# Moving the streamed tiles of the down and output projections by 64 bytes in SBUF

## The chip, the cores and the metric

The kernel runs on one core of a Trainium2 chip. The metric is device time in microseconds (us) of one execution; lower is better.

## What is computed

Two transformer blocks in a row on one sequence of 256 tokens with 1,024 features, all in float32. Cut to what matters here:

```python
def swiglu(h, w_gate, w_up, w_down):            # D_FF = 2816
    return (silu(h @ w_gate) * (h @ w_up)) @ w_down

def first_block(x, ...):                        # DEPTH = 2
    for i in range(DEPTH):
        x = x + 0.5 * swiglu(rms_norm(x, g[0]), ...)
        h = rms_norm(x, g[1])
        x = x + (even_mixer(h, ...) if i % 2 == 0 else mla_mixer(h, ...))
        x = x + 0.5 * swiglu(rms_norm(x, g[2]), ...)
        x = x + per_layer_embedding(rms_norm(x, g[3]), p[i], ...)
    return x

def second_block(x, ...):                       # one hybrid layer
    u = rmsnorm(x, g) @ w_in
    x = x + concat([attention(u), ssd(u), pooling(u)]) @ w_out
    x = x + swiglu(rmsnorm(x, g2), ...)
    return rmsnorm(x, norm_final)
```

Five feed-forward layers (SwiGLU) hold most of the arithmetic. Each of the three mixers ends in an output projection of 1,024 by 1,024.

## The kernel before

Activations lie transposed: a tile has 128 features on the partitions and the 256 tokens along the free dimension, so `x` is eight tiles of 128x256. Weights (220 pieces of 1 MB) stream from HBM through three buffers `wraw`, in the order in which they are used.

**Split operands.** Every float32 operand of a large product is split into two tiles of the type fp32r, a high part and the remainder. A product is then three matmuls that accumulate into the same PSUM region: high weight by high row, high weight by low row, low weight by high row. `load_piece` (lines 233 to 260) makes `whi` on ScalarE (line 256) and `wlo` on VectorE (line 257), half a piece at a time. Each buffer of `whi` and `wlo` is 128x1024, that is eight weight blocks of 128 columns (512 bytes per partition each).

**What is stationary and what streams.** All the matmuls of the large products go through `mm` (line 163). In `fm` (lines 327 to 385) and `out_proj` (lines 400 to 411) a 128x128 weight block is loaded as the stationary operand (a LDWEIGHTS instruction, engine PEld in the rows) and the 256 columns of a row tile stream past it (a MATMUL, engine PE). In `tm` (lines 387 to 398) it is the other way round: a block of the row tile is stationary and the weights stream, 512 columns at a time in most cases.

**Which row tiles there are.**
- `hh0` to `hh7` and `hl0` to `hl7`, the high and low parts of the normalized rows. They are the moving operand of the gate and up projections of all five feed-forward layers (1,056 matmuls each) and of the first projections of the mixers.
- `big`, a rotating set of 13 tiles of 128x1024. The gated rows of a feed-forward are written there, two blocks (high, low, high, low) to a tile (lines 445 to 450), and are the moving operand of the down projection: 22 blocks by 8 output blocks by 3, 528 matmuls per layer. The even mixer's output projection (8 by 8 by 3, 192 matmuls), the two small projections of the per-layer embedding (48 each) and five of the eight blocks of the hybrid layer's output projection (120) stream from `big` too.
- `o2`, three tiles of 128x512 with the rows of one attention head or pair (named `o` in the rows): the moving operand in the output projection of the attention layer (192) and in the other three blocks of the hybrid layer's (72).

**Addresses.** Three pools take SBUF one after the other: `wp` (weights), `cp` (constants, `x`, `hh`, `hl`), `sp` (working tiles). Inside a pool tiles are laid out in the order in which a name is first asked for, each rounded up to 32 bytes:

```python
        self.wp = pool("wp")          # L114
        self.cp = pool("cp")
        self.sp = pool("sp", 2)
        ...
        t = self.sp.tile([P, cols], dt, name="big", bufs=13)     # L129
```

From the sizes follow these byte addresses within a partition (the same on all 128):

| tiles | first address | bytes of one | start of every 512-byte block, modulo 512 |
|---|---|---|---|
| `whi`, `wlo` | 41,088 and 65,664 | 4,096 | 128 |
| `hh0`, `hl0`, ... `hl7` | 99,648 | 1,024 | 320 |
| `gu` (first name of `sp`) | 132,352 | 2,048 | 256 |
| `big` | 153,344 | 4,096 | 256 |
| `o2` | 209,664 | 2,048 | 256 |

So a streamed `hh` or `hl` tile starts 192 bytes behind a weight block, modulo 512, and a streamed `big` or `o2` tile 128 bytes behind one, whatever buffer and whatever block it is.

**Order around the change.** A framework schedules each engine's instructions and sets the semaphores. The order of the matmuls follows the code: in a feed-forward, two column pairs are accumulated block by block while the rows are still being normalized (the first 96 matmuls), the sum of squares is taken with four small matmuls on `sqa` (`Stat.begin`, line 69), 48 matmuls later two transposes of `ny` spread its inverse root over the partitions (`Stat.finish`, line 88), and the rest of gate and up follows without another kind of matmul; the down projection comes right behind.

Of the kernel before, what the change touches and what calls it, by code (L numbers as in the profile page):

```python
# [10 lines left out]
FT = mybir.dt.float32  # L11
# [6 lines left out]
P = 128  # L18
# [88 lines left out]
class Kern:  # L107
# [61 lines left out]
    def constants(self):  # L169
        nc, a, cp = self.nc, self.a, self.cp  # L170
        self.cols = cp.tile([P, a["cols"].shape[1]], FT, name="cols")
        self.x = []
        self.raw = [self.wp.tile([P, PIECE], FT, name="wraw", bufs=3) for _ in range(2)]

        def load_x(c, n, eng=nc.sync):
            t = cp.tile([P, n * T], FT, name=f"x{c}")
            eng.dma_start(t, a["xT"][:, c * T : (c + n) * T])
            self.x += [t[:, u * T : (u + 1) * T] for u in range(n)]

        def load_w(i, q, n):  # L180
            o = slice(q * 512, (q + n) * 512)
            nc.sync.dma_start(self.raw[i][:, o], a["wts"][i][:, o])


        self.ones = cp.tile([P, 1], FT, name="ones")
        nc.vector.memset(self.ones, 1.0)
        idle = self.tmp(512, "gu", bufs=3)
        nc.vector.memset(idle, 0.0)
        ps = self.aux()
        for _ in range(5):  # L190
            self.mm(ps[:, :T], idle[:, :P], idle[:, :T])
        load_x(0, 1)
        nc.scalar.dma_start(self.cols, a["cols"])
        load_w(0, 0, 1)
        load_x(1, 1, nc.scalar)
        load_w(0, 1, 1)
        load_x(2, 1, nc.scalar)
        load_w(0, 2, 1)
        load_x(3, 1)
        load_w(0, 3, 1)  # L200
        load_x(4, 2)
        load_w(1, 0, 2)
        load_x(6, 2)
        load_w(1, 2, 2)
        self.ident = cp.tile([P, P], FT, name="ident")
        nc.sync.dma_start(self.ident, a["ident"])
        self.hT = [
            (cp.tile([P, T], FR, name=f"hh{c}"), cp.tile([P, T], FR, name=f"hl{c}"))
            for c in range(D)
        ]  # L210
        self.eps = cp.tile([P, 1], FT, name="eps")
        nc.vector.memset(self.eps, EPS)
        nc.scalar.activation(self.tiny(1, "nz"), self.ones, AF.Silu)
# [1435 lines left out]
```

## Time and profile before

| | |
|---|---|
| median of 3 runs | 1348.85 us (1342.49 to 1348.98) |
| the profiled execution's own time | 1348.33 us |
| its span, first to last instruction | 1346.5 us |
| TensorE busy with matmuls | 1319.8 us of the span, 10,830 instructions |
| TensorE busy with weight loads | 1290.1 us (beside the matmuls) |
| VectorE, ScalarE, GpSimd busy | 920.6, 727.1, 76.7 us |
| read from HBM | 232.78 MB, 174 GB/s over the span |

The busy time of a matmul in the profile reaches from its issue to its modelled end, and the next one is issued long before that; so neither "busy" nor the mean duration of one (281 ns and the like) is the time that a matmul costs. In a stretch that holds matmuls of one kind and no pause, that cost is the step from one start to the next. It is had from a stretch of known length: the length, plus the duration of one (0.28 us, because matmuls that only reach into the stretch are counted as well), divided by the count.

### The profile page before, as it was taken

The numbers are of one execution on the slowest core, as the hardware profiler recorded it, in microseconds if no ns is written. First come the engines' busy times: TensorE is split into PE (matmuls) and PEld (weight loads), VectorE is DVE, ScalarE is ACT, GpSimd is POOL, SyncE is SP. The second block draws the span as 40 slices with busy tenths as digits, with TensorE's granted clock in tenths as the row PEclk, the third lists the DMA queues.
The fourth block names the chain that finished last, engine by engine and source line by source line (L and its number), as shares of the span: only waits on it lengthen the run. The fifth ranks groups of instructions, "written<-read, shape, count | busy, mean of one in ns | idle before, by whom it ended". The sixth has DMA issues, their size and how long they took to land.

```text
span 1346.5 us, 25894 instructions
## 1 busy us (share of the span) xinstructions
PE 1319.8 (98%) x10830; PEld 1290.1 (96%) x10830; DVE 920.6 (68%) x1528; ACT 727.1 (54%) x1110; POOL 76.7 (6%) x94
## 2 busy tenths in 40 slices
PE   8999999999999999999999899999998999999997
PEld 8999999899999999999999679999998998999997
DVE  6866567968667557866656767766558897866643
ACT  6655446546544456655445666544445675644442
POOL 4000010002000001000010002000002000200001
PEclk9999999999999999999999999999999999999998
DMA  8755455345555453655455324555545343555541
GB/s 313 261 192 205 175 191 186 103 159 182 188 187 198 171 205 126 220 188 188 160 187 193 118 72 148 189 188 188 183 163 188 126 167 119 185 188 188 188 159 61
DMA packets 34933, 235.50 MB, mean 175 GB/s; under 512 B 4016, under 2 KB 4784, under 8 KB 7168
## 3 DMA queue, kind: packets, MB, share of 16 engines
q1 hardware_dynamic: 32976, 229.98, 49.1%
q0 software_dynamic: 832, 2.47, 0.6%
q8 instruction: 85, 1.39, 0.4%
q10 hardware_dynamic: 1008, 1.40, 0.3%
q14 instruction: 32, 0.26, 0.1%
HBM read 232.78 MB, written 1.05 MB: 174 GB/s over the span
## 4 chain that ended last, share of the span: by engine, by line
PE 74%; DVE 5%; ACT 2%; issue 1%; DVEq 0%; ACTq 0%
PE acc L163 70%; PE aux L163 4%; DVE wlo L257 2%; PE aux L299 0%; DVE big L1172 0%; PE aux L1127 0%; ACT whi L256 0%; DVE qs L958 0%; DVE kv L958 0%; DVE big L511 0%; ACT ae L1119 0%; ACT big L946 0%; ACT at L1129 0%; DVE big L1494 0%; DVE nz L293 0%
## 5 line engine op out<-in xcount | busy, mean ns | idle before, releaser
L257 DVE TENSOR_TENSOR wlo<-wraw,whi 128x1024 fp32r<-128x1024 f32 (+1 forms) x440 | 530.3, 1219 | 270.1 <-ACT whi L256 177.0
L256 ACT ACTIVATE whi<-wraw 128x1024 fp32r<-128x1024 f32 (+1 forms) x440 | 451.7, 1048 | 319.3 <-PE acc L163 224.9
L163 PE MATMUL acc<-hh,whi 128*128 128x256 f32 x2192 | 330.7, 281 | 4.1 <-ACT hh L535 3.1
L163 PE MATMUL acc<-hl,whi 128*128 128x256 f32 x2192 | 329.6, 280 | 0.2 <-DVE hl L540 0.2
L163 PE MATMUL acc<-hh,wlo 128*128 128x256 f32 x2192 | 328.8, 280 | 0.2 <-DVE wlo L257 0.2
L163 PEld LDWEIGHTS acc<-hh,whi 128*128 128x128 f32 x2192 | 288.5, 189 | 5.8 <-ACT hh L535 3.8
L163 PEld LDWEIGHTS acc<-hh,wlo 128*128 128x128 f32 x2192 | 288.7, 189 | 0.8 <-DVE wlo L257 0.6
L163 PEld LDWEIGHTS acc<-hl,whi 128*128 128x128 f32 x2192 | 288.6, 189 | 0.4 <-DVE hl L540 0.4
L163 PE MATMUL acc<-big,whi 128*128 128x256 f32 x2032 | 277.9, 283 | 0.0
L163 PEld LDWEIGHTS acc<-big,whi 128*128 128x128 f32 x2032 | 261.6, 189 | 0.4 <-ACT big L267 0.2
L163 PE MATMUL acc<-big,wlo 128*128 128x256 f32 x1016 | 164.8, 283 | 0.0
L163 PEld LDWEIGHTS acc<-big,wlo 128*128 128x128 f32 x1016 | 139.8, 189 | 0.0
L315 POOL TENSOR_TENSOR sqa<-sqa,sq 128x256 f32<-128x256 f32 x72 | 65.5, 910 | 1135.8 <-ACT sq L314 1133.7
L426 DVE TENSOR_TENSOR gu<-acc,rb 128x512 f32<-128x512 f32 (+1 forms) x122 | 81.9, 678 | 51.9 <-PE acc L163 51.9
L270 ACT ACTIVATE hh<-x,cols 128x256 fp32r<-128x256 f32 x64 | 30.3, 503 | 84.2 <-DVE x L465 80.6
L267 ACT ACTIVATE big<-pr 128x256 fp32r<-128x256 f32 x114 | 45.9, 409 | 51.9 <-DVE pr L444 50.1
L442 ACT ACTIVATE sg<-gu 128x256 f32<-128x256 f32 x110 | 44.8, 411 | 38.7 <-DVE gu L426 38.5
L268 DVE TENSOR_TENSOR big<-pr,big 128x256 fp32r<-128x256 f32 x114 | 47.9, 426 | 20.3 <-ACT big L267 20.2
L444 DVE TENSOR_TENSOR pr<-sg,gu 128x256 f32<-128x256 f32 x110 | 45.4, 418 | 2.8 <-ACT sg L442 2.8
L271 DVE SCALAR_TENSOR_TENSOR hl<-x,cols,hh 128x256 fp32r<-128x256 f32 x64 | 36.9, 602 | 8.5 <-ACT hh L270 8.3
L163 PE MATMUL aux<-big 128*128 128x128 f32 (+5 forms) x260 | 37.6, 310 | 1.9 <-DVE big L680 1.7
L314 ACT ACTIVATE sq<-x 128x256 f32<-128x256 f32 x62 | 24.0, 405 | 24.9 <-DVE x L467 18.4
(297 smaller groups left out, 788.1 us busy)
## 6 DMA issues: line engine op xcount, KB each, us to landing
wraw<-wts SPq DMA_DIRECT2D x216, 1024.0 KB, 4.9
wraw<-wts SPq DMA_DIRECT2D x4, 256.0 KB, 5.0
wraw<-wts SPq DMA_DIRECT2D x2, 512.0 KB, 6.5
x<-xT SPq DMA_DIRECT2D x2, 256.0 KB, 5.7
big<-wsT POOLq DMA_DIRECT2D x1, 512.0 KB, 10.4
gu<-pT ACTq DMA_DIRECT2D x2, 256.0 KB, 3.1
out<-big SPq DMA_DIRECT2D x2, 256.0 KB, 2.2
out<-big ACTq DMA_DIRECT2D x2, 256.0 KB, 2.4
```

Source lines behind the costliest of these rows:

```text
L163: return self.nc.tensor.matmul(out, l, r, start=start, stop=stop, skip_group_check=True).ins
L256: nc.scalar.activation(hi[:, i], s, AF.Copy)
L257: nc.vector.tensor_tensor(lo[:, i], s, hi[:, i].bitcast(FT), op=OP.subtract)
L267: a = nc.scalar.activation(hi, src, AF.Copy)
L268: b = nc.vector.tensor_tensor(lo, src, hi.bitcast(FT), op=OP.subtract)
L270: a = nc.scalar.activation(hi, src, AF.Copy, scale=scale)
L271: b = nc.vector.scalar_tensor_tensor(lo, src, scale, hi.bitcast(FT), op0=OP.mult, op1=OP.subtract)
L314: nc.scalar.activation(q, src, AF.Square)
L315: self.mark = nc.gpsimd.tensor_tensor(self.sq[0], self.sq[0], q, op=OP.add).ins
L426: self.nc.vector.tensor_tensor(out.rearrange("p (u t) -> p u t", u=n), ps.rearrange("p (u t) -> p u t", u=n), rb.unsqueeze(1).to_broadcast ...
L442: self.mark = nc.scalar.activation(sg, gu[:, :T], AF.Silu).ins
L444: nc.vector.tensor_tensor(pr, sg, gu[:, T:], op=OP.mult)
```

## The change

One tile of 64 bytes per partition is asked for in the working pool, after `gu` and before every other name of that pool. Nothing reads or writes it.

```diff
@@ -208,6 +208,8 @@
             (cp.tile([P, T], FR, name=f"hh{c}"), cp.tile([P, T], FR, name=f"hl{c}"))
             for c in range(D)
         ]
+
+        self.sp.tile([P, 16], FT, name="pad", bufs=1)
         self.eps = cp.tile([P, 1], FT, name="eps")
         nc.vector.memset(self.eps, EPS)
         nc.scalar.activation(self.tiny(1, "nz"), self.ones, AF.Silu)
```

Every tile of `sp` but `gu` lies 64 bytes further on: `big` starts at 153,408 and `o2` at 209,728, both 320 modulo 512, and so do `sq`, `sqa`, `sg`, `pr`, `rb`, `ny`, `ae`, `at` and the other working tiles move by 64. The tiles of `wp` and `cp` (the weights, `x`, `hh`, `hl`, `ident`, the constants) stay where they were. A streamed `big` or `o2` tile now starts 192 bytes behind a weight block, modulo 512. The instructions of every engine and their order are the same as before.

## Rows read from the trace of the kernel before

**Rows 1.** The page: the span, and each engine's busy time.
```profile
span 1346.5 us, 25894 instructions
...
PE 1319.8 (98%) x10830; PEld 1290.1 (96%) x10830; DVE 920.6 (68%) x1528; ACT 727.1 (54%) x1110; POOL 76.7 (6%) x94
```
**Rows 2.** The page's costliest groups: busy us, mean ns | idle before, releaser.
```profile
L257 DVE TENSOR_TENSOR wlo<-wraw,whi 128x1024 fp32r<-128x1024 f32 (+1 forms) x440 | 530.3, 1219 | 270.1 <-ACT whi L256 177.0
...
L163 PE MATMUL acc<-big,whi 128*128 128x256 f32 x2032 | 277.9, 283 | 0.0
...
L163 PE MATMUL acc<-big,wlo 128*128 128x256 f32 x1016 | 164.8, 283 | 0.0
...
L444 DVE TENSOR_TENSOR pr<-sg,gu 128x256 f32<-128x256 f32 x110 | 45.4, 418 | 2.8 <-ACT sg L442 2.8
```
**Rows 3.** Stretches, PE alone: from:to, length, busy (count), granted clock, DMA share, GB/s.
```profile
40.00:120.00 80.00, 80.00 (x708) 1.00 0.63 218
132.00:190.00 58.00, 58.00 (x491) 1.00 0.52 182
216.00:236.00 20.00, 20.00 (x179) 1.00 0.61 211
...
340.00:420.00 80.00, 80.00 (x682) 1.00 0.54 185
435.00:495.00 60.00, 60.00 (x502) 1.00 0.49 170
...
950.00:1005.00 55.00, 55.00 (x461) 1.00 0.51 176
...
1276.00:1332.00 56.00, 56.00 (x469) 1.00 0.36 129
```
**Rows 4.** Timeline, PE, hybrid layer: weights stream past stationary rows. Start us, length, ...
```profile
1106.34 1.07 PE L163 MATMUL acc<-whi,hh 128*128 128x256 f32 x8
...
1109.06 1.07 PE L163 MATMUL acc<-whi,hh 128*128 128x256 f32 x8
```
**Rows 5.** Timeline, PE, start of the second feed-forward.
```profile
313.40 1.75 PE L163 MATMUL acc<-hh,wlo 128*128 128x256 f32 x14
314.99 0.50 PE L163 MATMUL aux<-ones,sqa 128*128 128x1 f32 x4
...
316.38 1.10 PE L163 MATMUL acc<-hl,whi 128*128 128x256 f32 x8
...
320.15 1.10 PE L163 MATMUL acc<-hh,wlo 128*128 128x256 f32 x8
```
**Rows 6.** Timeline, PE, first feed-forward, just behind its two transposes.
```profile
27.44 1.07 PE L163 MATMUL acc<-hl,whi 128*128 128x256 f32 x8
28.34 0.84 PE L163 MATMUL acc<-hh,wlo 128*128 128x256 f32 x6
```
**Rows 7.** Groups in the stretch 129.8 to 192.5 us: the first down projection.
```profile
L163 PE MATMUL acc<-big,whi 128*128 128x256 f32 x352 | 45.5, 281 | 0.0
L163 PE MATMUL acc<-big,wlo 128*128 128x256 f32 x176 | 25.6, 281 | 0.0
```
**Rows 8.** Groups of the whole span by shape: `o2` streamed; stationary `big`, 512 columns.
```profile
L163 PE MATMUL acc<-o,whi 128*128 128x256 f32 x176 | 34.2, 290 | 0.4 <-ACT o L267 0.4
...
L163 PE MATMUL acc<-whi,big 128*128 128x512 f32 x68 | 19.3, 405 | 1.7 <-DVE nz L293 1.1 <-DVE nz L292 0.6
```
**Rows 9.** Timeline, PE, 512 columns: past stationary `hh` and past stationary `big`.
```profile
206.19 2.00 PE L163 MATMUL acc<-whi,hl 128*128 128x512 f32 x8
208.03 1.99 PE L163 MATMUL acc<-wlo,hh 128*128 128x512 f32 x8
...
759.54 1.56 PE L163 MATMUL acc<-whi,big 128*128 128x512 f32 x6
760.94 0.86 PE L163 MATMUL acc<-wlo,big 128*128 128x512 f32 x3
```
**Rows 10.** Instructions on `ident`: transposes, ns min/median/max.
```profile
L1127 PEld LDWEIGHTS aux<-ident,ae x42: 137/140/143, 782.4 to 1131.7; 128*128 128x128 f32 x42
```

## The prediction

> **What bounds the kernel now.** The page comes first: TensorE is busy for 1319.8 of 1346.5 us [rows 1], so what a change is worth is what it takes from TensorE's stream of matmuls. The groups come next: 2,032 and 1,016 matmuls stream `big` [rows 2], and 176 stream `o2` past `whi` [rows 8], with half as many (88) past `wlo`. That is 3,312 matmuls with a moved tile, all 128x256. The groups give a mean of 283 ns each, which is overlap and no cost. The cost is in the view by stretches, which I read third: length plus 0.28 us, by the count.
>
> - Gate and up of the first feed-forward, `hh` and `hl` streamed: 80.28 us by 708 is 113.4 ns a matmul; its down projection, `big` streamed: 58.28 by 491 is 118.7 ns [rows 3].
> - Gate and up of the second feed-forward: 80.28 by 682 is 117.7 ns; its down projection: 60.28 by 502 is 120.1 ns. The fourth and fifth down projections: 55.28 by 461 is 119.9 ns and 56.28 by 469 is 120.0 ns [rows 3].
>
> TensorE has no idle time in any of these stretches and its clock is granted in full (1.00, the 2.4 GHz level), so neither a wait nor the clock makes the differences. The reader is to see two of them. One goes with the tile: 118.7 against 113.4, 120.0 against 117.7. The other goes with time: the same `hh` tiles against the same buffers take 113.4 ns in one stretch and 117.7 in another. I call these the **short** and the **long pace**.
>
> The pace changes where a stream is interrupted. In the second feed-forward 14 matmuls before the four on `sqa` take 1.59 us, 113.6 ns each; behind these four, 32 matmuls take 3.77 us, 117.8 ns each [rows 5], and that stays so for the stage. In the first feed-forward the pace behind the two transposes is the short one (8 in 0.90 us, about 113 ns [rows 6]). A down projection follows its gate and up without a pause and is at its own shorter pace (118.7) behind the short one and at its longer (120.0) behind the long one. So I read four numbers: tiles at distance 192 take 113.4 or 117.7, tiles at distance 128 take 118.7 or 120.0, and the pace is inherited.
>
> **Is it the distance?** Three other readings have to go first. That streaming from the region of `hh` is quick in itself: in the hybrid layer `whi` streams past stationary `hh`, 24 matmuls in 2.72 us, 113.3 ns [rows 4], so a tile of another pool at another offset streams just as quickly when its partner is `hh`. That it is the order of the matmuls: gate and up go through eight row blocks, the down projection through 22, and 118.7 and 120.0 stand there alike. That it is streaming alone: with `big` stationary and weights streaming 512 columns, 6 matmuls take 1.40 us, 233 ns, against 8 in 1.84 us, 230 ns, with `hh` stationary [rows 9]; the pair is the slower one in that direction too. What all quick pairs share is 192 bytes (or its reverse) and all slow pairs 128. What no row separates is that every slow pair has a tile of the working pool in it.
>
> **The change, part by part.**
>
> 1. *Removed and added instructions:* none, on any engine, and none moves; so no queue, wait or DMA is dealt with differently.
>
> 2. *The streamed tiles.* Taken at the pace that `hh` has at the same distance, each stage keeping the short or long pace that it is in:
>  - first down projection, 352 + 176 = 528 matmuls [rows 7], 118.7 to 113.4: 528 x 5.3 ns = 2.8 us;
>  - second down projection with the small projection of 48 behind it, 576, 120.1 to 117.7: 576 x 2.4 = 1.4 us;
>  - the other three down projections, 1,584, 120.0 to 117.7: 1,584 x 2.3 = 3.6 us;
>  - the even mixer's output projection, 192, which no long stretch of mine covers: it starts anew behind a pause, as the blocks do that take the short pace, so 192 x 5.3 = 1.0 us (0.4 at the long one);
>  - the remaining 432 (192 of the attention layer, 192 of the hybrid layer, 48 of the second small projection), cut up by transposes and scores: between 432 x 2.3 = 1.0 and 432 x 5.3 = 2.3 us, 1.6 taken. What of it lies under a head's softmax chain is worth nothing, so the low end is 0.
>
>  These sum to 10.4 us. In all the down projections TensorE's time is the path itself (no idle), and what follows each starts when its last matmul ends.
>
> 3. *Stationary `big`, 512 columns* (68 with `whi` streaming [rows 8], 34 with `wlo`): 102 x 3 ns = 0.3 us, 0 if hidden.
>
> 4. *Transposes.* `ident` stays and `ae`, `big`, `o` move under it. Their weight loads spread from 137 to 143 ns [rows 10]; the 42 of that row are the largest of several groups, some 150 in all, so up to 150 x 6 ns = 0.9 us either way. Taken as 0: at 128 columns nothing shows which relation is the worse.
>
> 5. *VectorE, ScalarE, GpSimd.* Pairs of operands change their relation too, such as `pr<-sg,gu`, where `sg` moves and `gu` stays (418 ns, 110 times [rows 2]). I know of no row that prices this. It is hidden under TensorE in the streams: `wlo` takes 1.22 us [rows 2] for eight weight blocks, which TensorE uses up in 24 matmuls or 2.7 us at 113.4 ns. Were 10 ns on each of the 110 uncovered, it would be 1.1 us. Taken as 0.
>
> 6. *The feed.* A down projection at 113.4 ns needs 64 KB per three matmuls, 65,536 B in 340 ns, 193 GB/s. The stretch of 40 to 120 us runs at that pace with 218 GB/s moved [rows 3], so the DMA follows.
>
> Sum: 10.4 + 0.3 = 10.7 us. Made against the profiled execution's own 1348.33 us, that is 1337.6 us; the median of the runs shown is 0.5 us higher, so I say **1338 us**, 0.8% under 1348.85. With the bounds of parts 2 to 5 the likeliest case reaches from 1334 to 1341.
>
> The Trainium skill speaks against all of it: "SBUF — State Buffer", section "Who interferes with whom", gives TensorE two independent read ports, one for the moving operand and one for the weight load, and says that PE never waits on anyone. By that rule the distance between the two operands could not matter, and the sum would be 0, 1348.3 us. The trace does not agree that nothing happens (113.4 against 118.7 ns in the same profile), but it does not show that the two reads are what collides.
>
> **The rivals.**
>
> - *The distance does nothing (chance 0.16).* The pace belongs to the working pool's place in SBUF, or to something else about these tiles. For it: no row parts pool from distance, and the rule just named. Against it: the quick stream of `whi` past `hh`, and the constancy of 118.7 and 120.0 over 13 buffers in 53 KB. That the change doesn't do what it says (the tile dropped, or rounded away) belongs here; 64 bytes are two of the allocator's steps of 32, so I give that next to nothing. Time: 1348.3 us, no change.
>
> - *More streams take the short pace (0.10).* The tiles around the interruptions (`sqa`, `ny`) move too, and the pace seems to be set by how a stream starts. If one of the four later feed-forwards turns, its gate and up gain 1,056 x 4.3 ns and its down projection as much for 528: 1,584 x 4.3 = 6.8 us, hence 1331 us; with all four, 1310. For it: the first feed-forward is in the short pace with the same code. One run of the three before is 6.4 us under the others, the size of one such turn. Against it: rows 5 have an entry that I see nothing of the move in, and the later four behave alike.
>
> - *The first feed-forward loses the short pace (0.08).* The same 6.8 us given back: 1344.5 us, within what counts as no change.
>
> - *Slower (0.04).* The distance does nothing and the move of `ny` and `sqa` turns the stretches that are short now into long ones. The place is the entry of a stream; the price is 4.3 ns for each `hh` matmul that is at the short pace: some 900 in the first feed-forward (103 us from its transposes to 129.8 us), some 350 in the even mixer, and the first 48 to 96 of every other stage, 600 in all; 1,850 x 4.3 = 8.0 us, and 1.4 ns (118.7 to 120.1) for the 720 matmuls of the first down projection and the even output, 1.0 us. That gives 1357.3 us, 0.6% slower. It decides only if nearly all these entries turn: 6.7 us, the bound of "slower", need over 1,500 matmuls.
>
> **How the numbers follow.** The forecast has 0.62. A measurement of this kernel can tell about 0.5%, 6.7 us, from no change; the forecast's 10.7 clears that by 4, and I take 0.02 of it as falling short through the scatter of the runs. Faster: 0.60 + 0.10 = 0.70. Same: 0.16 + 0.08 + 0.02 = 0.26. Slower: 0.04. The range takes in the likeliest case (1334 to 1341), one further turn of pace (1331), one lost (1344.5) and no effect at all (1348.3 to 1348.9): 1329 to 1349. Left out are several turns at once and the slower case, under 0.1.
>
> **What the profile of the changed kernel would show.** Right: the stretches of the down projections give about 113.4 ns behind a gate and up of 113.4 and about 117.8 behind 117.8, with no step where `big` takes over from `hh`; the stretches of gate and up are unchanged. The distance is refuted if the down projections stay at 118.7 and 120.0. If the total is off while these are right, the fault is in the inheritance: the stretches of gate and up from 30 to 130, 340 to 420, and those of the last three feed-forwards would show which pace each took. If TensorE shows idle time in a down projection, the feed was the limit after all.

## The result and the profile after

| | before | changed |
|---|---|---|
| median of 20 runs each | 1348.64 us | 1341.25 us |
| lowest to highest | 1342.49 to 1353.85 | 1331.63 to 1346.12 |
| the profiled execution, its span | 1348.33, 1346.5 | 1341.66, 1340.0 |

The ratio of the two sets of runs is 0.9936, with a 95% interval of 0.9918 to 0.9954: 8.6 us faster (6.2 to 11.1), 0.64%. The two medians alone lie 7.4 us apart. The forecast was 1338 us, faster by 10.7. A second set of runs of the same changed kernel, in the last experiments below, gave 0.9938 (0.9909 to 0.9967).

The page of the changed kernel, its span, its busy times and the two large groups that stream `big`, which answer to [rows 1, 2]:

```profile
span 1340.0 us, 25894 instructions
...
PE 1313.9 (98%) x10830; PEld 1283.5 (96%) x10830; DVE 922.5 (69%) x1528; ACT 727.4 (54%) x1110; POOL 76.7 (6%) x94
...
L163 PE MATMUL acc<-big,whi 128*128 128x256 f32 x2032 | 271.8, 280 | 0.0
...
L163 PE MATMUL acc<-big,wlo 128*128 128x256 f32 x1016 | 161.7, 280 | 0.0
```

The instructions are the same in number, the other engines are busy for as long as before, within 2 us, and TensorE still is for 98%. What changed is the pace. The view by stretches of the changed kernel, PE alone (columns as in [rows 3]: from:to, length, busy and count, granted clock, DMA share, GB/s):

```profile
40.00:120.00 80.00, 80.00 (x708) 1.00 0.63 216
132.00:188.00 56.00, 56.00 (x497) 1.00 0.54 189
...
340.00:420.00 80.00, 80.00 (x682) 1.00 0.55 190
430.00:490.00 60.00, 60.00 (x512) 1.00 0.51 178
...
950.00:1004.00 54.00, 54.00 (x460) 1.00 0.51 176
1270.00:1328.00 58.00, 58.00 (x495) 1.00 0.36 127
```

Length plus 0.28 us, by the count, as ahead of the prediction. Gate and up of the first two feed-forwards stand where they stood: 113.4 and 117.7 ns. The first down projection went from 118.7 to 113.2 ns, the second from 120.1 to 117.7, the fourth from 119.9 to 118.0, the fifth from 120.0 to 117.7. These are the short and the long pace, and each down projection has that of the gate and up ahead of it. The place where `big` takes over from `hh` shows no step any more. The timeline of the changed kernel there (start us, length us, engine, line, operation, tiles, shape, count):

```profile
128.22 1.07 PE L163 MATMUL acc<-hh,wlo 128*128 128x256 f32 x8
129.13 0.39 PE L163 MATMUL acc<-big,whi 128*128 128x256 f32 x2
...
129.47 0.39 PE L163 MATMUL acc<-big,whi 128*128 128x256 f32 x2
```

Eight with `hh` take 0.91 us, three with `big` 0.34: 113 ns on both sides of the takeover.

**Where the 6.5 us between the two spans come from.** The kernels have the same matmuls in the same order, so their starts can be paired. Counted from the first matmul of each part to the first behind it, the five down projections (with the 48 small matmuls behind the second) take 2.8, 1.3, 1.2, 1.2 and 1.2 us less, 7.6 in all. All matmuls that stream `big` or `o2`, these included, take 9.2 us less. Those that stream `hh` and `hl` take 0.3 less, the 512-column ones apart from the next paragraph 0.1 less. That would be 9.6; 3.0 us are given back at one place, and 0.1 among the small matmuls.

That place is the start of the attention layer, where `big` is stationary. First the timeline of the kernel before, then that of the changed one, at the same instructions:

```profile
740.23 1.43 PE L163 MATMUL acc<-whi,big 128*128 128x512 f32 x5
```

```profile
732.63 1.67 PE L163 MATMUL aux<-ones,gu 128*128 128x1 f32 x10
734.22 2.50 PE L163 MATMUL acc<-whi,big 128*128 128x512 f32 x5
```

Five matmuls of 512 columns reach over 1.43 us in the one and 2.50 in the other, and the clock says why. By stretches, the changed kernel (granted clock third from the end):

```profile
726.00:732.00 6.00, 6.00 (x55) 1.00 0.53 178
733.00:740.00 7.00, 7.00 (x22) 0.52 0.46 150
```

From about 733.3 us the clock is granted at 0.5, the 1.2 GHz level, until 740.1, and then in full again. Ahead of the fall TensorE had done two dozen matmuls of a single column (on `ones`; 14, then the 10 shown). The kernel before does the same ones and kept its clock of 1.00 in this execution. Such spells are not the change's own: all thirteen profiles, that of the kernel before included, have one at the start of the hybrid layer (6.8 or 10.2 us long) and one at their very end. A further one, of 3.4 or 6.8 us, is in eight of them, here or some 200 us earlier. The second profile of the changed kernel (e9) has it here too, from 733.3 us on, but 3.4 us long; those of the kernel before, e1, e2, e5 and e11 have none. So its length differs between executions of one kernel; whether its place does is not shown, and what sets one off was not tried.

### The profile page after: what moved, and what is told of

Read it like the earlier page. It is cut to its first block, busy times and chain, and to the rows that moved or that the text cites. A ratio compares the mean times of both kernels' runs of the same rounds, so it can differ in the third digit from the quotient of the medians.

```text
span 1340.0 us, 25894 instructions
## 1 busy us (share of the span) xinstructions
PE 1313.9 (98%) x10830; PEld 1283.5 (96%) x10830; DVE 922.5 (69%) x1528; ACT 727.4 (54%) x1110; POOL 76.7 (6%) x94
## 4 chain that ended last, share of the span: by engine, by line
PE 75%; DVE 4%; ACT 2%; issue 1%; DVEq 0%; ACTq 0%
PE acc L163 70%; PE aux L163 4%; DVE wlo L259 1%; ACT whi L258 0%; DVE big L1174 0%; PE aux L301 0%; PE aux L1129 0%; DVE qs L960 0%; ACT at L1131 0%; DVE big L1002 0%; ACT ae L1121 0%; ACT big L948 0%; DVE big L513 0%; DVE big L1496 0%; ACT hh L272 0%
## 5 line engine op out<-in xcount | busy, mean ns | idle before, releaser
L163 PE MATMUL acc<-big,whi 128*128 128x256 f32 x2032 | 271.8, 280 | 0.0
L163 PEld LDWEIGHTS acc<-big,whi 128*128 128x128 f32 x2032 | 256.6, 189 | 0.5 <-ACT big L269 0.2
L163 PE MATMUL acc<-big,wlo 128*128 128x256 f32 x1016 | 161.7, 280 | 0.0
## 6 DMA issues: line engine op xcount, KB each, us to landing
big<-wsT POOLq DMA_DIRECT2D x1, 512.0 KB, 10.7
```

The lines of the kernel that those rows point to most:

```text
L163: return self.nc.tensor.matmul(out, l, r, start=start, stop=stop, skip_group_check=True).ins
```

## The experiments

Theory D: the distance between the streamed tile and the weight block, modulo 512 bytes or a divisor of it, sets the price of a matmul. Theory R: the price belongs to the working pool, its region of SBUF, or to having been moved. Theory P stands beside D: which of the two paces a stream takes is set where it is entered, and inherited from then on. All edits below are shown against the changed kernel, but for that of e7, and cut to the lines that matter ("..." marks a cut); "pad" is the changed kernel's 64-byte tile. A number of ns per matmul is worked out from the stretch as above, or from two starts of a timeline. The kernels of e1, e2, e3, e6 and e7 were executed once each; with 11 us between executions of one kernel their times settle little, and it is their paces that carry the argument.

**e1. The same tiles, moved further, to a distance of 0 modulo 128.** `big` stands 256 bytes behind a weight block; a second tile in front of `o2` puts this one 320 bytes behind, 64 modulo 128.

```diff
-        self.sp.tile([P, 16], FT, name="pad", bufs=1)
+        self.sp.tile([P, 32], FT, name="pad", bufs=1)
...
+        self.sp.tile([P, 16], FT, name="opad", bufs=1)     # in front of o2
```

> The unused tile is 128 bytes instead of 64, and a second one of 64 bytes stands ahead of o2: big starts 256 bytes behind a weight block modulo 512 (0 modulo 128), o2 320 (64 modulo 128), hh and hl stay at 192. If the pace goes by the distance modulo 128: down projections at 118.7 behind a short-pace gate and up and 120.0 behind a long one, as before the change, with a step where big takes over; the attention layer's output projection (o2) at 113.3 or 117.8. If it goes by the place in the working pool, or by big having been moved at all: down projections at 113.3 or 117.8 again. If the period is 256 or 512: big differs from the kernel before, o2 from the changed one.

It took 1349.33 us (the kernel before beside it: 1348.67, median of 7). First and second down projection, by stretches:

```profile
132.00:190.00 58.00, 58.00 (x486) 1.00 0.52 182
...
435.00:495.00 60.00, 60.00 (x502) 1.00 0.49 170
```

119.9 and 120.1 ns: the gain is gone, though the tiles were moved and lie in the same pool. `o2` is the counterpart in the same kernel. Its matmuls in the attention layer's output projection, by the timeline of this kernel and then of the kernel before, first and last of a run of 36 steps:

```profile
818.76 0.40 PE L163 MATMUL acc<-o,whi 128*128 128x256 f32 x2
...
823.00 0.40 PE L163 MATMUL acc<-o,whi 128*128 128x256 f32 x2
```

```profile
818.28 0.41 PE L163 MATMUL acc<-o,whi 128*128 128x256 f32 x2
...
822.60 0.41 PE L163 MATMUL acc<-o,whi 128*128 128x256 f32 x2
```

4.24 us against 4.32, 117.8 ns against 120.0. In one program, from one pool, the tile at 64 modulo 128 is quick and the tile at 0 is slow: that is D, and R falls. One thing is off: behind a gate and up at 113.4 ns, `big` at 256 takes 119.9 ns and not the 118.7 that it takes at 128. So 128 and 256 are not quite alike.

**e2. The two kinds of tile exchange their distances.** A tile in front of `hh` in place of the pad moves `hh` to 256, `big` to 192, and `o2` to 448.

```diff
+        cp.tile([P, 16], FT, name="cpad")                  # in front of hh
...
-        self.sp.tile([P, 16], FT, name="pad", bufs=1)
...
+        self.sp.tile([P, 64], FT, name="opad", bufs=1)     # in front of o2
```

> An unused tile of 64 bytes ahead of hh0 in the constants' pool, and 256 bytes ahead of o2, none behind gu: hh and hl are at 256 (0 modulo 128), big at 192, o2 at 448 (64 modulo 128). If the distance decides: gate and up at 118.7 or 120.0 and down projections at 113.3 or 117.8, the reverse of the kernel before; with 6,576 matmuls on hh and hl about 15 to 25 us slower than the changed kernel. If what decides is something in the working pool: gate and up stay at 113.3 or 117.8, and the time is that of the changed kernel.

1348.79 us. Gate and up and the down projection of the first feed-forward, then of the second:

```profile
40.00:120.00 80.00, 80.00 (x669) 1.00 0.59 198
138.00:196.00 58.00, 58.00 (x514) 1.00 0.53 184
345.00:425.00 80.00, 80.00 (x669) 1.00 0.54 183
437.00:497.00 60.00, 60.00 (x532) 1.00 0.54 190
```

120.0 and 113.4, 120.0 and 113.3 ns. The order is reversed: `hh` pays now, and `big` does not. This is the plainest evidence for the distance. The pair in exchanged roles changed with it: in the hybrid layer `whi`, which did not move, streams past stationary `hh`, as in [rows 4]. The timeline of e2:

```profile
1107.87 1.12 PE L163 MATMUL acc<-whi,hh 128*128 128x256 f32 x8
...
1110.75 1.12 PE L163 MATMUL acc<-whi,hh 128*128 128x256 f32 x8
```

24 matmuls take 2.88 us, 120.0 ns, where they took 2.72 and 113.3. So it is not the address of the streamed tile by itself. What no run parts is the distance from the row tile's own address modulo 128, in either role: the weight buffers lie at 0 modulo 128 in every run.

The size was missed (7.5 us above the changed kernel's median, not 15 to 25), because the down projections took the short pace behind a slow gate and up. So a down projection does not simply go on in whichever pace came before it; that held only where both are at the good distance.

**e3 and e6. Other distances.** e3 puts `hh` and `o2` at 224 and `big` at 160, with a tile of 32 bytes in front of `hh`, one of 64 in front of `o2`, and no pad. e6 takes steps of 16 bytes: every `hh`, `hl` and `big` tile is made 128 bytes longer and used from its 16th byte on, which gives 80 for `hh`, 48 for `big` and 32 for `o2`, modulo 128 (modulo 512 the distance then differs from tile to tile); the small tiles are halved to make room, the pad is 32 bytes, and it also has the added matmul of e4.

```diff
-        t = self.sp.tile([P, cols], dt, name="big", bufs=13)
-        return t
+        t = self.sp.tile([P, cols + 32], dt, name="big", bufs=13)
+        return t[:, 4 : 4 + cols]
...
```

> 32 bytes ahead of hh0 and 64 ahead of o2: hh and hl at 224 (96 modulo 128), big at 160 (32 modulo 128), o2 at 224 like hh. If the distance decides, hh and o2 show the same paces, whatever these are; each theory of how it decides gives others: steps of 64 alone would leave hh at 113.3/117.8 and big at 118.7/120.0; a smooth course between 64 and 128 gives values between these two; a finer unit may give paces under 113.3 or above 120.

> With the matmul on ident, and with distances that are no multiple of 32: hh and hl 80, big 48, o2 32, all modulo 128 (the tiles are 128 bytes longer and used from 16 bytes on; the small tiles are cut to 64 bytes to make room). If the two reads collide in units of 64 or 32 bytes: hh as at 64 or 96 (113.3, or 118.3), big as at 32 or 64. If the pace goes smoothly with the distance from 64: hh and big alike, between 113.3 and 118.5. If 64 is not the best place, one of the two falls under 113.3, towards the 106.7 ns that 256 columns take at 2.4 GHz.

1355.19 and 1360.23 us. First gate and up and first down projection of e3, then of e6:

```profile
40.00:120.00 80.00, 80.00 (x679) 1.00 0.60 203
...
138.00:196.00 58.00, 58.00 (x491) 1.00 0.50 176
```

```profile
40.00:120.00 80.00, 80.00 (x677) 1.00 0.58 198
140.00:190.00 50.00, 50.00 (x429) 1.00 0.50 174
```

So, in ns a matmul, over all the large stages of these runs:

| distance modulo 128 | 0 | 32 | 48 | 64 | 80 | 96 |
|---|---|---|---|---|---|---|
| pace | 118.7 to 120.2 | 117.4 or 118.7 | 117.2 to 118.3 | 113.3 or 117.8 | 118.6 | 118.2 to 118.4 |

64 is the best of those tried, and the only one at which the short pace was seen. At the others gate and up took one pace in all five feed-forwards of a kernel, and its down projections differ by 1.5 ns at most (at 32 four took 118.7 and the third 117.4). `o2` in e3, at 96 as `hh` is, takes 118.1 ns (21 matmuls in 2.48 us).

**e4, e5 and e10. The other loss: the entry.** Four of five feed-forwards run at the long pace, which costs 1,584 x 4.4 ns = 7.0 us each. In [rows 5] the pace changes at four small float32 matmuls. e4 adds one float32 matmul of 128 columns behind the two transposes of `ny`, into a part of the PSUM tile that nothing reads; the output is the same.

```diff
-        self.pb = pb = k.aux()[:, :T]
+        full = k.aux()
+        self.pb = pb = full[:, :T]
...
+            if copy:
+                k.mm(full[:, T : T + P], k.ident, k.ident)
```

e5 is e4 without the pad, e10 is e4 once more, on another chip and with more runs.

> The changed kernel with one matmul more (ident by ident, float32, 128 columns, into an unread part of the PSUM tile) behind every pair of transposes of ny, that is ahead of the long streams. If the pace is set by how the stream is entered: the streams behind it take another pace than in the changed kernel, in most cases the short one, since five of six entries behind a float32 matmul were short in the two traces; four feed-forwards turned would give 4 x 6.8 = 27 us less, for 10 x 0.2 us more. If the pace is a matter of the stage, or of chance: the same four feed-forwards at 117.8, and 2 us more than the changed kernel.

> The kernel before with the matmul on ident behind the transposes of ny, and no unused tile: big and o2 stay at 128. If distance and entry are two separate things: gate and up at 113.3 as in the run before this one, the down projections at 118.7 behind them, so 3,312 x 5.3 ns = 17.6 us more than with the tile, about 1334 us; against the kernel before, some 14 us less. If the unused tile was needed for the entries to turn (through the tiles that it moves): gate and up stay at 117.8 in four feed-forwards, and the time is about that of the kernel before plus 2 us.

> The changed kernel with one float32 matmul on ident behind the transposes of ny, once more. If that matmul turns the entries as it did in all four executions of the first run: 113.3 in the gate and up and the down projections of all five feed-forwards, 1316 to 1318 us in every execution. If the first run was a matter of luck or of its chip, as the run with such a matmul in both places suggests: some feed-forwards at 117.8, executions spread over 1317 to 1345 us.

e4 took 1316.93 us in the median of 4 runs, 0.9769 (0.9732 to 0.9806) of the kernel before; e10 took 1318.13 in the median of 6, 0.9788 (0.9758 to 0.9818). Nine of the ten executions lie between 1316.2 and 1318.5 us, one at 1325.2, the price of one turn. The stretches of e4:

```profile
40.00:120.00 80.00, 80.00 (x708) 1.00 0.62 212
132.00:188.00 56.00, 56.00 (x496) 1.00 0.53 188
330.00:430.00 100.00, 100.00 (x885) 1.00 0.58 198
436.00:486.00 50.00, 50.00 (x443) 1.00 0.56 196
```

Every one of them gives 113.3 ns or nearly (113.4, 113.5, 113.3, 113.5), and so do those of the third, fourth and fifth feed-forward, left out here. The timeline of e10 at the second feed-forward shows the entry, with the added matmul, two instructions in the trace, in its first row:

```profile
318.32 0.39 PE L166 MATMUL aux<-ident 128*128 128x128 f32 x2
...
319.46 1.07 PE L166 MATMUL acc<-hl,whi 128*128 128x256 f32 x8
...
322.18 1.07 PE L166 MATMUL acc<-hl,whi 128*128 128x256 f32 x8
```

24 matmuls take 2.72 us behind it, 113.3 ns; in [rows 3], with no such matmul ahead, the same stage runs at 117.7.

e5 took 1331.62 us, 0.9888 (0.9836 to 0.9941). Its second gate and up, and first and second down projection:

```profile
132.00:190.00 58.00, 58.00 (x491) 1.00 0.52 181
330.00:430.00 100.00, 100.00 (x883) 1.00 0.59 200
440.00:490.00 50.00, 50.00 (x423) 1.00 0.52 180
```

`hh` runs at 113.6 and `big`, back at distance 128, at 118.7 and 118.9. So pace and distance are two things. With every feed-forward short the pad is worth 13.5 us (e5 against e10, on one chip) to 16 (0.9888 less 0.9769 of 1348), against 8.6 in the changed kernel: at the long pace the distance costs 2.3 ns a matmul, at the short one 5.4.

**e7 and e11. Other added matmuls at the same place.** e7 adds a third transpose in place of the float32 matmul (shown against e4), e11 two fp32r matmuls of 512 columns (weights streaming past a block of `hh`) into a tile that nothing reads (cut to the matmuls, which stand where e4 has its one).

```diff
-                k.mm(full[:, T : T + P], k.ident, k.ident)
+                k.bcast(full[:, T : T + P], self.r[:, 0:1].to_broadcast([P, P]))
```

```diff
+                z = k.aux()
+                for _ in range(2):
+                    k.mm(z, k.hT[0][0][:, :P], k.kw[:, :512])
```

> The changed kernel with a third transpose of ny where the other run has the float32 matmul: one instruction more of the kind that was there. If any additional instruction turns the entry (a matter of how many steps lie ahead): short paces as with the float32 matmul, about 1317 us. If it takes the float32 matmul, whose weight load is longer and which runs as two passes: four feed-forwards stay at 117.8, about 1342 us.

> In place of the float32 matmul on ident, two fp32r matmuls with hh0 stationary and 512 columns of whi streaming, into an unread PSUM tile: the kind that stands ahead of the long stream in the even mixer, which was at the short pace in every trace of a kernel with hh at 192. If such a matmul sets the pace of what follows: all feed-forwards at 113.3, 1317 to 1319 us in every execution. If the even mixer's stream is short for another reason: the entries vary as in the changed kernel, 1333 to 1347 us.

e7: 1341.94 us, with the first feed-forward long now (117.7 ns) and the second short (113.3): one of five, as in the changed kernel, but another one. By stretches:

```profile
40.00:120.00 80.00, 80.00 (x682) 1.00 0.59 201
...
340.00:430.00 90.00, 90.00 (x797) 1.00 0.58 199
```

e11: 1351.26 us, ratio 1.0025 (1.0000 to 1.0050), with all five feed-forwards long:

```profile
40.00:120.00 80.00, 80.00 (x682) 1.00 0.58 200
...
340.00:430.00 90.00, 90.00 (x767) 1.00 0.55 188
```

That was a miss with the sign reversed, 10 us above the changed kernel in the first set. Twenty matmuls of 512 columns were added in all, two at each of ten places, and cost some 5.4 us themselves (a pair takes 0.54 us in the timeline of this kernel); the first feed-forward's turn adds 7.0. What precedes a stream bears on its pace, but not by the rule "anything that keeps TensorE from the 256-column stream turns it short".

**e8 and e9. Is it the kind of matmul?** e8 adds the same float32 matmul at the four on `sqa` as well (`Stat.begin`), beside that of e4. e9 is the changed kernel once more, on the same chip as e8.

```diff
+            k.mm(ps[:, P : 2 * P], k.ident, k.ident)       # in Stat.begin, behind the small matmuls
```

> The changed kernel with the float32 matmul on ident behind the transposes of ny and behind the small matmuls on sqa as well. If the float32 matmul turns every entry that it stands ahead of: the blocks of 48 behind sqa go from 117.8 to 113.3 too (six of the ten were long in the run with one such matmul), 6 x 48 x 4.4 ns = 1.3 us less, for about 13 x 0.2 us = 2.6 us of added matmuls: 1316 to 1319 us, no gain over the run with one. If those entries are set otherwise: 2 us more.

> The changed kernel once more, beside the run above on the same chip. If the pace of each stream is drawn anew where it is entered: single stretches of gate and up or blocks of 48 at another pace than in its first profile, and runs apart by up to 14 us in steps of about 7; the down projections at 113.3 or 117.8, as their gate and up, in any case. If the paces belong to the program: the same pace in every stretch as in the first profile.

e8 took 1338.27 us (1331.47 to 1346.86, 10 runs) where 1316 to 1319 was expected: with a second matmul of the very kind that helped, the help is gone. (e8 and e9 ran on a third chip, where the kernel of e4 was not run; e4 and e10 gave the same on two others.) Gate and up of the second to the fifth feed-forward, from short to long and back:

```profile
330.00:420.00 90.00, 90.00 (x797) 1.00 0.58 196
550.00:640.00 90.00, 90.00 (x766) 1.00 0.56 192
840.00:920.00 80.00, 80.00 (x708) 1.00 0.57 198
1160.00:1240.00 80.00, 80.00 (x681) 1.00 0.56 189
```

113.3, 117.9, 113.4, 117.9 ns. e9 took 1338.30 us (1332.34 to 1344.74, 10 runs; before beside it 1347.25), and its profile shows other feed-forwards short than that of the first profile of the same kernel. The first three gate and up:

```profile
40.00:120.00 80.00, 80.00 (x681) 1.00 0.60 201
...
340.00:420.00 80.00, 80.00 (x708) 1.00 0.57 193
560.00:640.00 80.00, 80.00 (x681) 1.00 0.56 197
```

117.9, 113.4 and 117.9 here; 113.4, 117.7 and 117.7 before. The down projections behind them are at 117.6, 113.2 and 117.6, so they inherit as forecast. One and the same program thus takes the short pace now in one feed-forward, now in another. That the runs of one kernel spread over 11 to 15 us is of the size of one or two such turns; that the spread is made of them is inferred from two profiles of the changed kernel, from the executions of e4 and e10, where it all but vanishes with the turns, and from those of e11, which fall into two groups, 1345.4 to 1347.2 and 1351.2 to 1354.0 us.

**What stays open.** Which sequence ahead of a stream gives which pace: one float32 matmul behind the transposes gave short nearly always, one there and one at `sqa` gave a mixture, two fp32r matmuls of 512 columns gave long in the profile taken. Why a distance costs what it costs: no run looks into SBUF. Whether it is the distance or the row tile's own address modulo 128: a run with the weight buffers moved by 64 bytes would tell, and none was made. Why 128 and 256 differ behind a short gate and up.

The best version is e4: the 64-byte tile and the added matmul, 1317 to 1318 us, 2.1 to 2.3% under the kernel before and 1.5 to 1.7% under the change alone.

## Why the prediction was right, point by point

1. *What bounds the kernel.* Right: with the other engines unchanged, what TensorE saved is what the program saved.

2. *The streamed tiles of the down projections.* Right in kind and size: 7.8 us forecast (2.8, 1.4 and 3.6), 7.6 measured (2.8, 1.3 and 3.5). The first went to the short pace and the others to the long one, each as its gate and up. That "each stage keeping the short or long pace that it is in" came out stage by stage is luck: the two profiled executions drew the same paces in all five feed-forwards, and the second profile of the changed kernel (e9) drew others.

3. *The output projections and small ones.* These are the terms that were mis-sized: 1.0 us forecast for the even mixer and 1.6 for the remaining 432, 0.5 and 1.0 measured by the paired starts. The premise "it starts anew behind a pause, as the blocks do that take the short pace" held for one piece and failed for the others. The even mixer's longest piece, 120 matmuls, did take the short pace. The timeline of the kernel before, then of the changed one, first and last of a run of 84 steps:

```profile
293.54 0.40 PE L163 MATMUL acc<-big,whi 128*128 128x256 f32 x2
...
303.51 0.40 PE L163 MATMUL acc<-big,whi 128*128 128x256 f32 x2
```

```profile
290.17 0.39 PE L163 MATMUL acc<-big,whi 128*128 128x256 f32 x2
...
299.69 0.39 PE L163 MATMUL acc<-big,whi 128*128 128x256 f32 x2
```

9.97 us against 9.52, 118.7 ns against 113.3; the other 36, with the entry among them, gave only 0.05 more, and the whole piece went from 14.37 us to 13.87. The 62 ahead of it took the long pace and went from 7.32 to 7.27 only. The longest piece of the hybrid layer, also 120, went from 14.35 to 14.24: from 118.7 ns, the quicker of the two paces at the old distance, to 117.8, the slower of the two at the new one. Where the pace is drawn at the entry, an analogy with other entries carries little.

4. *Stationary `big`.* 0.3 us forecast, 0.1 measured outside the half-clock spell. The term took the 3 ns between the two pairs of [rows 9] for the price of the distance at 512 columns; e2 does not bear that out, where `hh` at 0 modulo 128 is passed in 227 ns (16 matmuls in 3.63 us) and not in more than 230. Transposes, VectorE and the feed cost nothing, as taken: 189 GB/s were moved in the first down projection at 113.2 ns.

5. *What was missing.* No term stood for the clock. The profiled execution gave back 3.0 us in the half-clock spell, and that, with the 1.0 us of point 3, makes up the 4.0 us by which its 6.7 (1348.33 to 1341.66) fall short of 10.7; the smaller misses cancel. Over the 20 runs each the gain is 8.6 us by the ratio and 7.4 between the medians, where the profile shows 9.6 without the spell.

6. *The distance against the rule on ports.* The Trainium skill, "SBUF — State Buffer", section "Who interferes with whom", has TensorE's two read ports independent and PE waiting on nobody. The measurements decide otherwise for this stream: e2 gave 120.0 ns to `hh` and 113.4 to `big` by exchanging nothing but their addresses. They do not say that the ports are what collides.

7. *The rivals.* "The distance does nothing" is refuted by e1 and e2. "More streams take the short pace" and "the first feed-forward loses it" were told as things that the move might do. They are real turns, of the size given (6.8 us forecast, 7.0 by e4's and e10's paces), but they happen without a move: between two executions of the changed kernel (e9), and, as far as its spread of 11 us tells, in the kernel before too. That the later four feed-forwards "behave alike" was an accident of one profile, and "the pace is inherited" is half of the story: between two stages at the good distance it is, and the entry draws it.

## What to carry to other kernels

Where TensorE is busy throughout, work out the time per matmul stage by stage from stretches of the trace and compare stages that should cost the same: two per cent here lay in the addresses of two operands and in what stood ahead of a stream, and no wait shows either. Exchange the placement of two operands as a test before believing it, and look at several distances; in this kernel 64 bytes modulo 128 was the one that ran at 113 ns. If executions of one kernel scatter by more than half a per cent, compare the paces of the same stage in two profiles before comparing medians.

## What was unexpected of the hardware

- The same instructions at the same addresses run at 113.3 or at 117.8 ns for a hundred microseconds on end, and one added float32 matmul (two instructions in the trace, 0.14 us) in each of ten places was worth 20 to 24 us (1316.93 or 1318.13 against 1341.25 or 1338.30). The Trainium skill, "TensorE: Matmul & The Clock Gate", section "Back-to-back issue gap", gives columns by 2.4 GHz plus 2.5 ns for the isolated gap, an estimate of 109.2 ns at 256 columns; no stretch read here goes below 113.2.
- The two losses overlap. At the long pace the distance of 128 costs 2.3 ns a matmul, at the short one 5.4 (e5).
- Spells at half the granted clock, some 3 to 10 us long, stand in every profile between the long streams, and one at the same place had another length in another execution (6.8 and 3.4 us in the changed kernel); the one of 6.8 us read here cost 3.0 us.
